# A two-layer streaming encoder: the high parts of the prompt's queries and of the differential attention's keys and values cast by POOL in place of ACT

## The chip, the core and the metric

One Trainium2 chip, of which the kernel uses one core. A core has TensorE (PE in the profile; PEld is its loading of weights), VectorE (DVE), ScalarE (ACT), GpSimd (POOL) and a queue that issues transfers (SP). Each engine takes its own instructions in order. The metric is the device time of one execution in microseconds (us); smaller is better.

## What is computed

The reference runs two layers over 1024 prompt tokens and over 8 x 16 new tokens ("decode" below) with caches. Layer A has differential attention of 4 heads, with two score maps each, and cross-attention to 256 memory tokens; layer B has sliding-window attention with sinks and the same cross-attention. Every branch is gated, the branches go through one output projection, and a layer norm follows.

```
def diff_attend(q, k, v, mask, lam):
    s = jnp.einsum('bqhcd,bkhcd->bhcqk', q, k).astype(jnp.float32) * (DA_QK ** -0.5)
    ...
    p = jax.nn.softmax(s, axis=-1)
    a = p[:, :, 0] - lam * p[:, :, 1]
    return jnp.einsum('bhqk,bkhd->bqhd', a.astype(v.dtype), v)
```

Everything is float32, and the product must be about as precise. The kernel makes such a product from operands of a shorter type (`F32R`): an operand x is written as a high part, x cast to that type, and a low part, x minus the high part, and a product is the sum of two or three products of parts.

## The kernel before

Each operand is split by `split(hi, lo, src, eh, el)`: one engine casts `src` to `hi` (`eh`: "act" or DVE), another subtracts `hi` from `src` into `lo` (`el`: "dve" or "pool"). Weights and caches come from memory raw (`wraw`, `draw`), are cast by ACT and subtracted by DVE (`wh`/`wl`, `dkh`/`dkl`). What POOL subtracts is, above all:

- `load_q` and `mem_prompt`: the queries of one unit, loaded into `ldq` (128 x 256) and split into `qh` and `ql`; 96 such splits in a run.
- `build_head`: keys and values of a head of layer A, loaded into one of two `ldk` buffers (128 x 256). `stack_k` casts all 128 rows of a key tile into `kh` and overwrites the lower 64 rows with the low part; the values are split into the two halves of a `vh` tile.
- `layer_b_build`: the keys of layer B, also by `stack_k`, in four pieces of 64 x 512 out of two `P0` buffers; its values are split by ACT and POOL.

A unit of attention (`diff_prompt`, `mem_prompt`, `swa_prompt`) is a generator: it loads its queries, then makes scores (`sc`), exponentials (`P`, ACT), transposes (`tp`), splits those (`ah`, `al`) and multiplies by the values. `pipe` runs some 4 to 7 units in turn. Between their steps `dose` and `steps` emit background work, the projections (`pj`, three matmuls for each of 8 pieces of the contraction), and a second stream computes the decode attention (`dc`, `do`), whose queries are laid out by POOL's copies into `qc` and `qbd`.

This emission is not the final order. Class `Order` takes all instructions with their dependences, gives each a cost by a formula, and plans each engine's order with a list scheduler in four passes; `keep` fixes the best order found, engine by engine. The formula knows POOL's copies, its subtracts and that some instructions of DVE and POOL hold one another. An instruction that moves to another engine therefore changes the planned order on all of them, SP's transfers included.

Line numbers of the profile are those of the kernel before: L110 is the cast on ACT in `split`, L113 the subtract, L525 and L526 the two of `stack_k`, L184 the matmuls of the projections, L126 those of `mm`, L130 the transposes, L454 and L461 the loads of keys and values, L396 the loads of queries.

Of the kernel before, what the change touches and what calls it, by code (L numbers as in the profile page):

```python
# [64 lines left out]
class Kernel:  # L65
# [41 lines left out]
    def split(self, hi, lo, src, eh="act", el="dve"):  # L107
        nc = self.nc
        if eh == "act":
            nc.scalar.copy(hi, src)  # L110
        else:
            nc.vector.tensor_copy(hi, src)
        (nc.vector if el == "dve" else nc.gpsimd).tensor_tensor(lo, src, hi, op=ALU.subtract)  # L113
# [276 lines left out]
    def load_q(self, l, pair, t):  # L390

        self.need((("q", l), t // 3))
        x = self.t2([128, 256], "ldq").rearrange("p (a b) -> p a b", b=128)
        src = self.q[l][pair * 128:(pair + 1) * 128, t * 128:(t + 1) * 128].rearrange("(c d) t -> d c t", d=64)
        for i in range(2):
            self.nc.sync.dma_start(x[64 * i:64 * i + 64], src)  # L396
        qh, ql = self.q_tiles()
        self.split(qh, ql, x, "act", "pool")
        return [(qh[:, c], ql[:, c]) for c in range(2)]

    def load_q8(self, l, j):
# [120 lines left out]
        return [self.t2([128, 2, 128], x, F32R, bufs=2) for x in ("qh", "ql")]  # L522

    def stack_k(self, dst, x):
        self.nc.scalar.copy(dst, x)  # L525
        self.nc.gpsimd.tensor_tensor(dst[64:128], x[64:128], dst[64:128], op=ALU.subtract)  # L526


# [281 lines left out]
    def build_head(self, i):  # L810

        Kh, V = [None, None], [None, None]
        p, h = i // 2, i % 2

        def fill():
            hc = slice(h * 128, (h + 1) * 128)
            for half in (1, 0):
                if i:
                    yield from self.since(8 * i - (7 if half else 4))
                Kh[half] = self.kv_tile("kh", [128, 2, 512])  # L820
                V[half] = self.kv_tile("vh", [128, 4, 2, 128])
                for j in (0, 2):
                    t = 4 * half + j
                    self.need((("kvA", p), t + 1))
                    for c in range(2):
                        rows = slice(h * 128 + c * 64, h * 128 + c * 64 + 64)
                        x = self.load_k(("kvA", p), rows, slice(t * 128, t * 128 + 256), self.t2([128, 256], "ldk"))
                        self.stack_k(Kh[half][:, c, j * 128:j * 128 + 256], x)
                        if c:
                            yield  # L830
                    x = self.load_v(("kvA", p), t, 2, hc, self.t2([128, 256], "ldk"))
                    vt = V[half][:, j:j + 2]
                    self.split(vt[:, :, 0, :], vt[:, :, 1, :], x, "act", "pool")
                    yield

        return Kh, V, self.side(fill())
# [70 lines left out]
    def mem_prompt(self, l, h, pr, built):  # L907

        nc = self.nc
        self.phase(("m", l))  # L910
        mk, mv, build = built
        tok = slice(pr * 256, (pr + 1) * 256)
        self.need((f"mq{l}", h))
        x = self.reload_T((f"mq{l}", h), "ldq", tok)[:, 0, :]
        qh, ql = self.q_tiles()
        self.split(qh, ql, x.rearrange("p (a b) -> p a b", b=128), "act", "pool")
        yield
        while not mk:
            build.advance(1)
        sc = self.ps("sc")  # L920
        for i in range(2):
            self.mm3(sc[:, i * 256:(i + 1) * 256], qh[:, i, :], ql[:, i, :], mk[0][:, h, :], mk[1][:, h, :])
        self.dose()
        nmx = self.t2([128, 4], "nmx4", bufs=2)[:, 0:2]
        nc.vector.tensor_reduce(nmx, sc[:, 0:512].rearrange("p (a b) -> p a b", b=256), axis=AX.X, op=ALU.max, negate=True)
        P = self.t2([128, 1024], "P0")
        s = self.t2([128, 4], "s4", bufs=2)[:, 0:2]
        for i in range(2):
            nc.scalar.activation(P[:, i * 256:(i + 1) * 256], sc[:, i * 256:(i + 1) * 256], AF.Exp, bias=nmx[:, i:i + 1], accum_out=s[:, i:i + 1])
        r = self.t2([128, 4], "r4", bufs=2)[:, 0:2]  # L930
        nc.vector.reciprocal(r, s)
        for i in range(2):
            nc.scalar.activation(P[:, i * 256:(i + 1) * 256], P[:, i * 256:(i + 1) * 256], AF.Copy, scale=r[:, i:i + 1])  # L933
        yield
        build.flush()
        self.need((f"mg{l}", h))
        u = self.reload_T((f"mg{l}", h), "ldu", tok)[:, 0, :]
        ah, al = self.split_T([P[:, i * 256 + kb * 128:i * 256 + (kb + 1) * 128] for kb in range(2) for i in range(2)], 0.5)
        o = self.ps("tp")[:, 0:256]
        for kb in range(2):  # L940
            vt, q2 = mv[kb][:, h], slice(2 * kb, 2 * kb + 2)
            self.mm3(o, vt[:, 0, :], vt[:, 1, :], ah[:, q2], al[:, q2], start=(kb == 0), stop=(kb == 1))
        self.dose()
        yield
        mixp = self.t2([128, 256], "mixp")
        nc.vector.tensor_tensor(mixp, o, u, op=ALU.mult)
        nc.sync.dma_start(self.mixm[l][pr][:, h, :], mixp)
# [874 lines left out]
```

## Time and profile before

| what | value |
|---|---|
| median of 3 runs (lowest to highest) | 1151.73 us (1150.84 to 1156.75) |
| profiled execution, own time | 1155.46 us |
| its span, first to last instruction | 1153.7 us |
| mean granted TensorE clock | 0.996 of full speed |
| busy: PE / DVE / ACT / POOL | 97% / 71% / 63% / 30% of the span |

The table's last line is an average over stages: setup, the first projections and the first head's keys to about 90 us, layer A with the decode attention to about 600, output projection and norm to about 735, layer B to about 1040, and the last projection. Matmuls are pipelined and their ends are modelled, so the share of PE says little about short waits. In the rows further down, "out<-in" names tiles with their numbers left out, and a time in us counts from the start of the span.

### The profile page before, as it was taken

To read this page: it belongs to the slowest core of one execution; us is meant where nothing else is said; L and a number is where in the kernel's file an instruction comes from. 1 tells how busy PE (TensorE), PEld (TensorE's weight loads), DVE (VectorE), ACT (ScalarE), POOL (GpSimd) and SP (SyncE) were. 2 spreads that over 40 slices of the span, in tenths; PEclk is the share of its full clock that TensorE was granted. 3 is DMA by queue.
4 is the path that set the end of the run, shared out by engine and by line. 5 is a ranking of instruction groups with operands and counts; after the bars stand their busy time and mean duration, and the time that the engine had idled before them with its cause. 6 is when DMAs were issued, how large, how long until landed. Compare 5 with 4: busy or idle time off the path is not lost.

```text
span 1153.7 us, 21451 instructions
## 1 busy us (share of the span) xinstructions
PE 1118.5 (97%) x6404; PEld 992.1 (86%) x6404; DVE 821.2 (71%) x2084; ACT 728.9 (63%) x1863; POOL 349.8 (30%) x570
## 2 busy tenths in 40 slices
PE   8998999999999999999999999999999999999997
PEld 5798998789888987899778889999999999997885
DVE  4326898789999999997875488142657687675376
ACT  5327587677878887887874234332767788697111
POOL 3225434335332421221121144320323232125033
PEclk9999999999999999999999999999999999999999
DMA  8865656774787657777787654554433346678643
GB/s 281 221 177 150 185 173 192 188 228 142 233 273 223 189 181 244 220 245 222 207 258 226 231 192 141 150 146 135 150 114 118 121 141 210 200 222 243 208 167 136
DMA packets 206836, 221.67 MB, mean 192 GB/s; under 512 B 47088, under 2 KB 138224, under 8 KB 206704
## 3 DMA queue, kind: packets, MB, share of 16 engines
q1 hardware_dynamic: 206720, 220.31, 62.8%
q8 instruction: 50, 0.82, 0.3%
q14 instruction: 66, 0.54, 0.2%
HBM read 162.42 MB, written 58.72 MB: 192 GB/s over the span
## 4 chain that ended last, share of the span: by engine, by line
PE 71%; DVE 9%; DMA 8%; ACT 5%; issue 4%; SPq 1%; POOL 1%; DVEq 0%; ACTq 0%; POOLq 0%
PE pj L184 50%; PE tp L126 5%; PE sc L126 4%; PE do L126 4%; PE tp L130 4%; PE dc L126 3%; DVE dkl L113 2%; DVE wl L113 1%; DMA draw<-dk 1%; ACT ob L726 1%; DMA ldk<-kT_kvA 1%; DVE m L551 1%; DMA wraw<-wO 1%; PE dc L130 1%; DVE dP L638 1%
## 5 line engine op out<-in xcount | busy, mean ns | idle before, releaser
L184 PE MATMUL pj<-wh,th 128*128 128x512 f32 (+1 forms) x648 | 233.9, 362 | 5.9 <-ACT th L110 5.4
L184 PE MATMUL pj<-wl,th 128*128 128x512 f32 (+1 forms) x648 | 233.9, 362 | 0.2 <-POOL wl L113 0.2
L184 PE MATMUL pj<-wh,tl 128*128 128x512 f32 (+1 forms) x648 | 233.1, 360 | 0.0
L184 PE MATMUL pj<-th,wh 128*128 128x384 f32 x672 | 230.4, 343 | 0.2 <-ACT ev L374 0.2
L184 PE MATMUL pj<-th,wl 128*128 128x384 f32 x672 | 229.7, 342 | 0.0
L184 PE MATMUL pj<-tl,wh 128*128 128x384 f32 x672 | 229.0, 341 | 0.0
L113 DVE TENSOR_TENSOR dkl<-draw,dkh 128x512 fp32r<-128x512 f32 (+1 forms) x197 | 136.7, 703 | 23.6 <-ACT dkh L110 21.4
L113 POOL TENSOR_TENSOR ql<-ldq,qh 128x256 fp32r<-128x256 f32 x96 | 74.2, 777 | 248.8 <-ACT qh L110 195.3
L184 PEld LDWEIGHTS pj<-wh,th 128*128 128x128 f32 x648 | 122.3, 189 | 25.3 <-ACT th L110 5.7
L184 PEld LDWEIGHTS pj<-wl,th 128*128 128x128 f32 x648 | 122.1, 188 | 20.5 <-POOL wl L113 1.4
L110 ACT CAST wh<-wraw 128x512 fp32r<-128x512 f32 x160 | 98.6, 622 | 62.7 <-PE pj L184 40.7
L184 PEld LDWEIGHTS pj<-wh,tl 128*128 128x128 f32 x648 | 122.2, 189 | 18.6 <-DVE tl L113 0.9
L110 ACT CAST dkh<-draw 128x512 fp32r<-128x512 f32 (+1 forms) x197 | 119.6, 619 | 25.8 <-PE dc L126 8.4
L113 DVE TENSOR_TENSOR wl<-wraw,wh 128x512 fp32r<-128x512 f32 x156 | 109.8, 715 | 33.3 <-ACT wh L110 33.1
L184 PEld LDWEIGHTS pj<-th,wh 128*128 128x128 f32 x672 | 126.9, 189 | 2.4 <-ACT ev L374 0.5
L184 PEld LDWEIGHTS pj<-tl,wh 128*128 128x128 f32 x672 | 126.7, 188 | 1.8
L184 PEld LDWEIGHTS pj<-th,wl 128*128 128x128 f32 x672 | 126.8, 189 | 1.2
L126 PE MATMUL sc<-kh,qh 128*128 128x256 f32 (+2 forms) x224 | 68.9, 315 | 2.6 <-ACT P L559 1.4
L130 PE MATMUL tp<-ident,P 128*128 128x128 f32 x408 | 69.1, 275 | 1.3 <-DVE s4d L995 0.4
L126 PE MATMUL sc<-kh,ql 128*128 128x256 f32 (+2 forms) x224 | 68.1, 314 | 0.0
L559 ACT ACTIVATE P<-sc,m 128x512 f32<-128x512 f32 (+3 forms) x96 | 55.4, 581 | 8.9 <-DVE m L555 4.1
L130 PEld LDWEIGHTS tp<-ident,P 128*128 128x128 f32 x408 | 49.1, 140 | 9.5 <-ACT P L933 1.4
(235 smaller groups left out, 2369.6 us busy)
## 6 DMA issues: line engine op xcount, KB each, us to landing
draw<-dk SPq DMA_DIRECT2D x64, 256.0 KB
draw<-dv SPq DMA_DIRECT2D x64, 256.0 KB
ldq<-q SPq DMA_DIRECT2D x128, 64.0 KB
wraw<-wM SPq DMA_DIRECT2D x32, 256.0 KB
wraw<-wO SPq DMA_DIRECT2D x32, 256.0 KB
draw<-cmk SPq DMA_DIRECT2D x32, 256.0 KB
draw<-cmv SPq DMA_DIRECT2D x32, 256.0 KB
wraw<-wBT SPq DMA_DIRECT2D x24, 256.0 KB
```

Of the source, the lines that this page charges most:

```text
L110: nc.scalar.copy(hi, src)
L113: (nc.vector if el == "dve" else nc.gpsimd).tensor_tensor(lo, src, hi, op=ALU.subtract)
L126: self.last = self.nc.tensor.matmul(*args, **kw).ins.name
L130: self.last = self.nc.tensor.transpose(out, in_, self.ident[:k, :k]).ins.name
L184: ins = self.nc.tensor.matmul(*args, **kw).ins
L551: nc.vector.tensor_reduce(m2[:, i:i + 1], sc[:, :kn], axis=AX.X, op=ALU.max, negate=True)
L559: nc.scalar.activation(pt[:, 512 * i:512 * i + kn], sc[:, :kn], AF.Exp, bias=nmx, accum_out=st[:, i:i + 1])
L638: self.nc.vector.tensor_tensor_reduce(out, o, x, -1.0, TOP, ALU.add, ALU.min, nm)
L726: nc.scalar.activation(y[at], x[of], AF.Copy, scale=w[of])
```

## The change

In `split` a third choice for `eh` lets POOL make the high part. Four places use it: `load_q`, the values in `build_head`, the queries in `mem_prompt`, and (written out) `stack_k`, which layer B's keys use too. The subtract was on POOL and stays there, so POOL makes the cast and then the subtract. Nothing else in the program is edited: the splits of weights, caches, probabilities, memory keys and values, and of layer B's values are as before.

```diff
@@ -108,6 +108,8 @@
         nc = self.nc
         if eh == "act":
             nc.scalar.copy(hi, src)
+        elif eh == "pool":
+            nc.gpsimd.tensor_copy(hi, src)
         else:
             nc.vector.tensor_copy(hi, src)
         (nc.vector if el == "dve" else nc.gpsimd).tensor_tensor(lo, src, hi, op=ALU.subtract)
@@ -395,7 +397,7 @@
         for i in range(2):
             self.nc.sync.dma_start(x[64 * i:64 * i + 64], src)
         qh, ql = self.q_tiles()
-        self.split(qh, ql, x, "act", "pool")
+        self.split(qh, ql, x, "pool", "pool")
         return [(qh[:, c], ql[:, c]) for c in range(2)]
 
     def load_q8(self, l, j):
@@ -522,7 +524,7 @@
         return [self.t2([128, 2, 128], x, F32R, bufs=2) for x in ("qh", "ql")]
 
     def stack_k(self, dst, x):
-        self.nc.scalar.copy(dst, x)
+        self.nc.gpsimd.tensor_copy(dst, x)
         self.nc.gpsimd.tensor_tensor(dst[64:128], x[64:128], dst[64:128], op=ALU.subtract)
 
 
@@ -830,7 +832,7 @@
                             yield
                     x = self.load_v(("kvA", p), t, 2, hc, self.t2([128, 256], "ldk"))
                     vt = V[half][:, j:j + 2]
-                    self.split(vt[:, :, 0, :], vt[:, :, 1, :], x, "act", "pool")
+                    self.split(vt[:, :, 0, :], vt[:, :, 1, :], x, "pool", "pool")
                     yield
 
         return Kh, V, self.side(fill())
@@ -913,7 +915,7 @@
         self.need((f"mq{l}", h))
         x = self.reload_T((f"mq{l}", h), "ldq", tok)[:, 0, :]
         qh, ql = self.q_tiles()
-        self.split(qh, ql, x.rearrange("p (a b) -> p a b", b=128), "act", "pool")
+        self.split(qh, ql, x.rearrange("p (a b) -> p a b", b=128), "pool", "pool")
         yield
         while not mk:
             build.advance(1)
```

The two added lines shift every later line: from L110 on, a line of before is two lines further down afterwards (the cast in `split` on POOL is L112, the subtract L115; those of `stack_k` L527 and L528). How the planner's orders differ is shown at three places. In the names a number tells tiles apart.

The first is POOL at the start of layer A, where the first head's keys (`kh_737`, out of `ldk`) are made ready, and behind them the decode queries `qc`. Before:

```order
60 L526 TENSOR_TENSOR kh_737<-ldk_739,kh_737 64x256
61 L526 TENSOR_TENSOR kh_737<-ldk_744,kh_737 64x256
62 L677 COPY qc_154_898<-qT_150_888 64x2x32 x2
63 L677 COPY qc_155_899<-qT_151_889 64x2x32 x2
64 L676 COPY qbd_902<-qT_150_888 64x2x2x16 x2
65 L676 COPY qbd_902<-qT_151_889 64x2x2x16 x2
66 L113 TENSOR_TENSOR ql_885<-ldq_881,qh_884 128x256
```

With the change:

```order
66 L527 CAST kh_737<-ldk_739 128x256
67 L528 TENSOR_TENSOR kh_737<-ldk_739,kh_737 64x256
68 L527 CAST kh_737<-ldk_744 128x256
69 L528 TENSOR_TENSOR kh_737<-ldk_744,kh_737 64x256
70 L679 COPY qc_154_898<-qT_150_888 64x2x32 x2
71 L679 COPY qc_155_899<-qT_151_889 64x2x32 x2
72 L678 COPY qbd_902<-qT_150_888 64x2x2x16 x2
73 L678 COPY qbd_902<-qT_151_889 64x2x2x16 x2
74 L112 CAST qh_884<-ldq_881 128x256
75 L112 CAST vh_738<-ldk_749 128x2x128
76 L115 TENSOR_TENSOR ql_885<-ldq_881,qh_884 128x256
```

Each subtract has its cast in front of it, in pairs, and the copies into `qc` still come behind the same two subtracts; the query's subtract `ql_885` has a value's cast ahead of it as well.

The second is TensorE at the same time: `dc_914` are the matmuls that read `qc`, and `pj` are projections of 384 columns. Before:

```order
375 L184 MATMUL pj_1124<-th_117,wl_642 128x384
376 L126 MATMUL dc_914<-qT_150_888,qc_154_898 128x64
377 L126 MATMUL dc_914<-qT_151_889,qc_154_898 128x64
378 L184 MATMUL pj_1124<-th_117,wh_641 128x384
379 L184 MATMUL pj_1124<-tl_118,wh_641 128x384
380 L184 MATMUL pj_1124<-th_117,wl_642 128x384
381 L184 MATMUL pj_1124<-th_117,wh_641 128x384
382 L184 MATMUL pj_1124<-tl_118,wh_641 128x384
383 L184 MATMUL pj_1124<-th_117,wl_642 128x384
384 L184 MATMUL pj_1124<-th_117,wh_641 128x384
385 L126 MATMUL dc_914<-qT_150_888,qc_155_899 128x64
```

With the change, from the same row on:

```order
375 L186 MATMUL pj_1124<-th_117,wl_642 128x384
376 L186 MATMUL pj_1124<-th_117,wh_641 128x384
377 L186 MATMUL pj_1124<-tl_118,wh_641 128x384
378 L186 MATMUL pj_1124<-th_117,wl_642 128x384
379 L186 MATMUL pj_1124<-th_117,wh_641 128x384
380 L186 MATMUL pj_1124<-tl_118,wh_641 128x384
381 L186 MATMUL pj_1124<-th_117,wl_642 128x384
382 L186 MATMUL pj_1124<-th_117,wh_641 128x384
383 L186 MATMUL pj_1124<-tl_118,wh_641 128x384
384 L128 MATMUL dc_914<-qT_150_888,qc_154_898 128x64
385 L128 MATMUL dc_914<-qT_151_889,qc_154_898 128x64
```

The matmuls that read `qc_154` stand 8 projection matmuls further back.

The third is ACT in layer A, at about 305 us of the profiled execution: `ah_4276` is the high part of a transposed tile that TensorE multiplies next, `P_1051` exponentials of the next map. Before:

```order
408 L615 ACTIVATE tp_4024,ss_4252<-tp_4024 128x128
409 L110 CAST ah_4276<-tp_4271 128x512
410 L110 CAST vh_3768<-ldk_3779 128x2x128
411 L110 CAST vh_3768<-ldk_3992 128x2x128
412 L110 CAST wh_4375<-wraw_4377 128x512
413 L110 CAST wh_4408<-wraw_4410 128x512
414 L110 CAST wh_4414<-wraw_4416 128x512
415 L110 CAST qh_4648<-ldq_4645 128x256
416 L559 ACTIVATE P_1051_4510,s_1052_4511<-sc_4505,m_1049_4504 128x256
```

With the change:

```order
359 L589 ACTIVATE mixp_4249<-tp_4024,r_905_4021 128x128
360 L561 ACTIVATE P_984_4311,s_985_4312<-sc_4306,m_982_4305 128x384
361 L110 CAST ah_4276<-tp_4271 128x512
362 L561 ACTIVATE P_1051_4510,s_1052_4511<-sc_4505,m_1049_4504 128x256
363 L708 COPY xs_4146<-dc_4328 64x512
364 L617 ACTIVATE tp_4024,ss_4252<-tp_4024 128x128
```

The two value casts and the query cast are gone from ACT, three weight casts have moved elsewhere, and the exponential of `P_1051` follows `ah_4276` at once.

## Rows read from the trace of the kernel before

**Rows 1.** The page's busy time of each engine, share of the span, instructions.

```profile
PE 1118.5 (97%) x6404; PEld 992.1 (86%) x6404; DVE 821.2 (71%) x2084; ACT 728.9 (63%) x1863; POOL 349.8 (30%) x570
```

**Rows 2.** Per stretch: length, busy PE PEld DVE ACT POOL, clock, DMA share, GB/s.

```profile
100.00:600.00 500.00, 484.86 (x2830) 424.01 (x2828) 447.02 (x1239) 398.26 (x1021) 155.55 (x259) 1.00 0.70 211
...
280.00:480.00 200.00, 192.92 (x1073) 166.68 (x1072) 191.09 (x575) 170.43 (x441) 60.09 (x87) 0.99 0.70 218
...
760.00:1040.00 280.00, 278.04 (x1781) 266.65 (x1779) 180.06 (x496) 198.36 (x565) 69.39 (x132) 1.00 0.51 156
```

**Rows 3.** Waits of TensorE's weight loads, 100 to 600 us: sum, times, longest.

```profile
PEld tp L126 <- ACT ah L110: 5.9, 11, 1.5
...
PEld sc L126 <- ACT P L559: 3.3, 6, 1.6
...
PEld tp L126 <- ACT ah L606: 2.1, 3, 1.4
...
PEld dc L126 <- ACT dkh L110: 2.1, 5, 1.0
...
PEld dc L130 <- DVE dP L727: 4.2, 4, 2.2
...
PEld tp L126 <- DVE al L113: 3.4, 8, 0.7
```

**Rows 4.** ACT's instructions by shape: count, busy us, mean ns, idle before.

```profile
L110 ACT CAST qh<-ldq 128x256 fp32r<-128x256 f32 x96 | 38.5, 407 | 22.5 <-PE sc L126 9.1 <-DMA ldq<-q 7.4 <-issue 4.6
...
L525 ACT CAST kh<-ldk 128x256 fp32r<-128x256 f32 x32 | 12.5, 406 | 9.8 <-DMA ldk<-kT_kvA 9.8
...
L110 ACT CAST vh<-ldk 128x256 fp32r<-128x256 f32 x16 | 6.4, 406 | 3.8 <-DMA ldk<-v_kvA 3.8
```

**Rows 5.** 100 to 600 us: qh (PE, PEld, ACT, POOL), ldk (ACT, POOL).

```profile
100.00:600.00 500.00, 44.02 (x150) 27.06 (x150) 17.83 (x44) 35.90 (x44) 1.00 0.70 211
...
100.00:600.00 500.00, 14.23 (x37) 31.06 (x37) 1.00 0.70 211
```

**Rows 6.** POOL's copies and DVE's subtracts: min/median/max ns; then DVE's by shape.

```profile
L677 POOL CAST qc<-qT x32: 229/234/1272, 90.9 to 409.4; 64x64 fp32r<-64x64 f32 x32
...
L731 POOL COPY Pn<-Pn x8: 196/270/715, 127.5 to 518.0; 128x16 f32<-128x16 f32 x8
...
L113 DVE TENSOR_TENSOR dkl<-draw,dkh x197: 443/684/1550, 18.1 to 1047.9; 128x512 fp32r<-128x512 f32 x194, 128x432 fp32r<-128x432 f32 x2, 128x288 fp32r<-128x288 f32 x1
...
L113 DVE TENSOR_TENSOR dkl<-draw,dkh 128x512 fp32r<-128x512 f32 x194 | 134.3, 701 | 23.5 <-ACT dkh L110 21.4 <-DMA ldu<-pre_mg_T 0.5 <-DMA om<-ob 0.3
...
L113 DVE TENSOR_TENSOR wl<-wraw,wh 128x512 fp32r<-128x512 f32 x156 | 109.8, 715 | 33.3 <-ACT wh L110 33.1
```

**Rows 7.** Start of layer A: chain, POOL's and TensorE's timeline, busy time behind it.

```profile
86.39 2.29 DMA ldk<-kT_kvA
...
89.24 1.59 POOL L526 TENSOR_TENSOR kh<-ldk,kh 64x256 fp32r<-64x256 f32 x2 [3.63 <-ACT kh L525]
...
90.89 1.07 POOL L677 CAST qc<-qT 64x64 fp32r<-64x64 f32 x4
...
91.45 0.41 PE L126 MATMUL dc<-qT,qc 128*128 128x64 f32 x2 [2.81 <-POOL qc L677]
...
92.70:96.00 3.30, 3.30 (x11) 2.75 (x9) 0.89 (x4) 1.94 (x5) 3.10 (x6) 0.50 0.30 80
```

**Rows 8.** Start of layer B: chain, TensorE's timeline, POOL's key subtracts.

```profile
750.34 0.96 POOL kh L526
...
751.30 4.82 DMA P<-ropeT
...
770.76 32.30 PE pj L184 x186
...
768.22 0.30 PE L126 MATMUL sc<-kh,qh 128*128 128x128 f32 x1 [1.05 <-ACT qh L110]
...
L526 POOL TENSOR_TENSOR kh<-P,kh x4: 1289/1294/1470, 747.8 to 751.6; 64x512 fp32r<-64x512 f32 x4
```

## The prediction

> **What bounds the kernel now.** I read the page's busy shares first, then the table by stage, then the waits of TensorE, and last the chain at the two places where a stage begins. TensorE is busy 97% of the span [rows 1], but its ends are modelled, so the share hides short waits. By stage [rows 2] the picture splits. From 760 to 1040 us (layer B) TensorE is busy 278.04 of 280 us: what other engines do there can hardly move the end. From 100 to 600 us (layer A with the decode work woven in) it is busy 484.86 of 500, and two other engines are close behind: DVE 447.02 and ACT 398.26, against POOL's 155.55. Between 280 and 480 us DVE is at 191.09 of 200 us, so DVE is as full as TensorE there, and ACT is at 170.43. The waits of TensorE's weight loads in 100 to 600 us [rows 3] say who comes last: the four longest that ACT ends sum to 5.9 + 3.3 + 2.1 + 2.1 = 13.4 us, the two longest of DVE to 4.2 + 3.4 = 7.6 us. So ACT is the engine most often late, DVE the one with least room. The change takes from ACT and gives to POOL; the question is whether POOL's new work costs DVE.
>
> **What moves, and its price.** ACT loses 96 casts of the prompt's queries (38.5 us), 32 of the keys (12.5) and 16 of the values (6.4) [rows 4], 57.4 us, and four wider key casts in layer B besides. POOL gets all of them. No row shows POOL casting 256 columns from 32 bits. Below, it can't be cheaper than POOL's cast of 64 columns, 229 ns at its shortest; above, it has one input where POOL's subtract of as many columns has two, and two of those take 1.59 us [rows 7], 0.80 each. The line through POOL's copy of 16 columns (196 ns) and its cast of 64 (229 ns) [rows 6] climbs 33 ns over 48 columns, 0.69 ns each, and gives 229 + 192 x 0.69 = 361 ns. I take 0.36 us: 144 x 0.36 = 52 us, and about 0.54 us for each of the four wide ones, 54 us in all, so POOL goes from 350 to some 404 us. A high part is thus made about as fast as on ACT (406 ns a cast), only on another engine.
>
> **Term 1: ACT's relief, -2.7 us.** In 100 to 600 us, 44 query casts (17.83 us) and 37 key and value casts (14.23) leave ACT [rows 5], 32.1 of its 398.26. Its load falls from 0.80 to 0.73. If the 13.4 us of waits [rows 3] fall with the load, by 8%, that is 1.1 us; if they fall like busy over idle time (0.80/0.20 = 3.9 to 0.73/0.27 = 2.7, by 31%) it is 4.2 us. I take 2.7, between them; the ends are 0 (DVE is late just behind ACT, as it can be between 280 and 480 us) and 4.2. The piece of ACT's order shown under the change is how this comes about: behind `ah_4276`, whose kind TensorE waits for most, ACT had two value casts, three weight casts and a query cast before its next exponential; now that exponential is next.
>
> **Term 2: the start of layer A, -1.4 us.** At 88.6 us TensorE runs into `dc_914` and waits 2.81 us for the `qc` copies on POOL, which stand behind two key subtracts [rows 7]; after it the granted clock is 0.50 for 3.3 us, the lower of the two levels (1.2 GHz). On POOL before: the keys' load ends at 86.39 + 2.29 = 88.68, ACT casts, the two subtracts run from 89.24 to 90.83, the copies follow. With the change, from about 88.8: two casts and two subtracts in a row, 2 x 0.36 + 1.59 = 2.31, to 91.1, so `qc` is ready some 0.3 us later. But TensorE's new order puts 8 more projection matmuls ahead of `dc_914`; at 32.30 / 186 = 0.174 us each [rows 8] they fill 1.4 us of the hole. The work moved ahead is taken from later, so it is a gain only as long as later has no hole for it, and the weave has such work throughout. Ends: -3.1, if the slower clock goes too (half of 3.3 us), and +1.0, if the loads of keys and values slip: they have two buffers, SP's next load waits for the subtract that frees one, and a pair of casts now stands on POOL in front of it (0.7 us a pair, where ACT made one while POOL subtracted).
>
> **Term 3: DVE held by POOL, +1.3 us.** DVE's subtract `dkl` takes 684 ns in the median and 1550 at most [rows 6]; POOL's 64-column cast 234 and 1272: each is now and then held by the other. The price over the whole run: 194 `dkl` with a mean of 701 lose 17 ns each, 3.3 us; 156 `wl` of the same shape with a mean of 715 lose 31 each, 4.8 us. So 8.1 us of DVE's time for 350 us of POOL's, 2.3%; 54 us more cost 1.3 us, and as DVE has no room between 280 and 480 us I count all of it. Ends: 0, and what the first rival says.
>
> By the Trainium skill (SBUF — State Buffer, section Who interferes with whom) a DVE instruction with two SBUF inputs and a GpSimd instruction that reads SBUF share a read interface, and whichever comes second is fully blocked until the other ends. The two maxima agree with it. Taken as the price, it would cost a meeting the rest of a cast, and the sum would then be the first rival's and not this one's; the measured mean is far below.
>
> **Term 4: the start of layer B, +0.4 us.** There POOL's four 512-column key subtracts (1.29 us each) are on the chain, and with them the release of the buffers that the rotary tables are loaded into (4.82 us), at whose end TensorE waits 1.05 us for a query's cast [rows 8]. Two casts of 0.54 stand in front of the first pair, where one ACT cast (two of the 406 ns ones at most, as it has twice the columns) stood ahead of it: the first buffer comes free 0.3 to 0.5 us later, and the second, behind four casts, 1.4. I take 0.4; ends 0 (the load of the tables may stand behind another transfer in SP's order) and 1.4.
>
> **At nothing:** the change issues no DMA itself. The query casts in layer B (TensorE full there; without that cover they would gain a little of ACT's time), and the wait of POOL's queue on loads: a cast that waits for its load now holds POOL's queue, where before the subtract behind it held it just as long, waiting for ACT.
>
> **Sum:** -2.7 - 1.4 + 1.3 + 0.4 = -2.4 us. The profiled execution took 1155.46 us, 3.7 above the median of the three runs; it would go to 1153.1, and a median of 1151.73 to 1149.3.
>
> **The rivals.** A difference under about 0.5% (5.8 us) can't be told from none, so the forecast is "no change": chance 0.42.
> *Slower: POOL's casts block DVE.* Place: 100 to 600 us, above all 280 to 480, where a DVE delay goes straight into TensorE's waits. If each of the 81 casts there holds a subtract for half its length, 0.18 us, DVE loses 14.6 us; with terms 1, 2 and 4 the sum is -2.7 - 1.4 + 0.4 + 14.6 = +10.9, 1162.6. It decides from a mean hold of (5.8 + 3.7) / 81 = 0.12 us. For it: the maxima of [rows 6]. Against it: POOL works already 155.55 of these 500 us, and a `dkl` loses 17 ns in the mean. Chance 0.22.
> *Faster: ACT's lateness was the cause of more.* If half of the 13.4 us go, and the start of layer A gains its 3.1, then -6.7 - 3.1 + 1.3 + 0.4 = -8.1, 1143.6. It decides from 4.4 us of those waits gone, a third. For it: ACT ends more of TensorE's waits than DVE does, and DVE's own waits on ACT shrink too; ACT no longer waits at the head of its queue for keys that are being loaded. Against it: DVE's 191.09 of 200. Chance 0.36.
>
> All engines' orders are remade by the planner, which adds a few us to either side. The likeliest time is 1149.3. The range for 8 in 10 goes from 1137 to 1161, across both rivals' times but for the slow one's last; the forecast's own is 1146 to 1157.5. The chances of faster, the same and slower are those of the three cases: 0.36, 0.42, 0.22.
>
> **What would show it.** ACT busy near 669 and POOL near 404 us; 144 casts of 256 columns on POOL near 0.36 us; `dkl` with a mean under 0.71; the wait ahead of `dc` near 91 us about 1.4 us long; the waits on `ah` and `P` in 100 to 600 us shorter by a fifth. A `dkl` mean above 0.75, or TensorE waiting for POOL's `qh`, `ql` or `kh` for some us, would prove me wrong on the slow side; waits on `ah` halved, on the fast side.

## The result: slower by 0.9%, outside the range

| kernel | median | lowest to highest | runs |
|---|---|---|---|
| before, beside it | 1153.12 us | 1150.84 to 1156.75 | 4 |
| with the change | 1164.99 us | 1162.48 to 1166.38 | 4 |

The ratio is 1.0089 with a 95% interval of 1.0067 to 1.0111, some 10 us (the two medians stand 11.9 us apart, which lies within it). The profiled execution took 1165.36 us. Below are the lines of its profile that answer to the rows of before. First the page's busy times [rows 1]:

```profile
PE 1120.1 (96%) x6404; PEld 991.9 (85%) x6404; DVE 833.9 (72%) x2084; ACT 683.6 (59%) x1715; POOL 423.8 (36%) x718
```

The instructions moved as the change says: 148 from ACT to POOL. ACT lost 45.3 us of busy time; the rows that left it sum to some 60, but ACT's instructions overlap a little in the records, and busy time counts such stretches once. POOL gained 74.0. DVE has the same 2084 instructions and is busy 12.7 us longer: they got slower.

The windows of [rows 2], and below them 300 to 400 us, of after; columns as there:

```profile
100.00:600.00 500.00, 478.46 (x2791) 418.97 (x2790) 447.83 (x1226) 368.63 (x927) 197.46 (x340) 1.00 0.70 208
280.00:480.00 200.00, 189.06 (x1051) 160.38 (x1051) 192.23 (x569) 154.37 (x395) 77.09 (x126) 1.00 0.69 210
760.00:1040.00 280.00, 276.79 (x1762) 265.62 (x1761) 183.26 (x486) 179.96 (x506) 95.24 (x182) 1.00 0.51 154
...
300.00:400.00 100.00, 92.85 (x497) 77.42 (x497) 94.43 (x276) 73.47 (x187) 41.95 (x68) 1.00 0.74 226
```

The same 100 us of before:

```profile
300.00:400.00 100.00, 97.86 (x546) 87.30 (x546) 95.47 (x288) 85.34 (x222) 33.56 (x45) 0.98 0.75 232
```

TensorE is busy 6.4 us less in layer A's 500 us, and 5.0 of these are lost between 300 and 400, where DVE was full before the change and still is. TensorE runs 497 matmuls there instead of 546, and DVE 276 instructions in 94.4 us instead of 288 in 95.5; as the order was remade, they aren't the same ones. ACT has 26 us of room there now and nothing comes of it. Layer B's 280 us lose another 1.3. The granted clock is 1.00 in all four rows of the changed kernel (the full level, 2.4 GHz).

The waits of TensorE's weight loads from 100 to 600 us, as in [rows 3] (ACT's cast in `split` keeps its line number, L110; `ah` of L606 is now L608):

```profile
PEld tp L128 <- DVE al L115: 6.3, 12, 2.0
PEld tp L128 <- ACT ah L110: 4.1, 6, 1.7
PEld tp L132 <- ACT tp L617: 3.7, 3, 2.1
PEld tp L128 <- ACT ah L608: 3.1, 3, 1.8
PEld do L128 <- DVE dP L115: 2.7, 4, 1.0
PEld tp L132 <- DVE P L574: 2.6, 3, 1.5
...
PEld sc L128 <- ACT P L561: 2.0, 6, 0.7
```

The four longest that ACT ends sum to 12.9 us against 13.4, the two longest of DVE to 9.0 against 7.6. Some of ACT's waits shrank (`ah` of L110 5.9 to 4.1, `P` 3.3 to 2.0) and others of ACT came in their place (`ah` of L608 2.1 to 3.1, `tp` 1.3 to 3.7).

The casts on POOL and DVE's two large subtracts by shape [rows 4, 6], busy us and mean ns behind the bar:

```profile
L112 POOL CAST qh<-ldq 128x256 fp32r<-128x256 f32 x96 | 43.2, 451 | 206.3 <-PE sc L128 181.0 <-issue 10.1 <-DMA ldq<-q 9.1
L527 POOL CAST kh<-ldk 128x256 fp32r<-128x256 f32 x32 | 16.5, 518 | 24.5 <-DMA ldk<-kT_kvA 24.4
L112 POOL CAST vh<-ldk 128x256 fp32r<-128x256 f32 x16 | 9.6, 602 | 13.7 <-DMA ldk<-v_kvA 10.2 <-PE tp L128 3.4
L115 DVE TENSOR_TENSOR dkl<-draw,dkh 128x512 fp32r<-128x512 f32 x194 | 137.6, 718 | 24.0 <-ACT dkh L110 17.6 <-PE dc L128 3.1 <-DMA mixm<-mixp 1.0
L115 DVE TENSOR_TENSOR wl<-wraw,wh 128x512 fp32r<-128x512 f32 x156 | 110.6, 719 | 37.0 <-ACT wh L110 35.1 <-DMA ldu<-pre_gs_T 1.4
```

The same casts as one tile's instructions (shortest, median, longest ns):

```profile
L112 POOL CAST qh<-ldq x96: 387/397/901, 91.3 to 1044.3; 128x256 fp32r<-128x256 f32 x96
...
L527 POOL CAST kh<-ldk x32: 390/398/1832, 67.5 to 410.0; 128x256 fp32r<-128x256 f32 x32
...
L527 POOL CAST kh<-P x4: 611/616/959, 755.2 to 760.1; 128x512 fp32r<-128x512 f32 x4
```

A cast of a query takes 0.397 us in the median (0.36 was predicted); means of 0.451 to 0.602 and a longest one of 1.832 say that some of POOL's casts are held, too. With the four wide ones they come to 72 us, not 54.

The start of layer A in the timeline (start, us; in brackets the wait ahead and what ended it), with the window behind it, as in [rows 7]:

```profile
88.93 1.18 POOL L679 CAST qc<-qT 64x64 fp32r<-64x64 f32 x4
...
89.79 0.30 PE L128 MATMUL dc<-qT,qc 128*128 128x64 f32 x2
...
95.52 0.67 PE L128 MATMUL sc<-kh,qh 128*128 128x512 f32 x1 [1.82 <-POOL kh L528]
...
92.70:96.00 3.30, 1.48 (x8) 1.07 (x7) 1.99 (x4) 0.84 (x2) 3.15 (x6) 0.95 0.16 52
```

The wait of 2.81 us ahead of `dc` is gone, and the stretch of half clock behind it too (0.95 in the same window, against 0.50). A wait of 1.82 us for a key on POOL has come 4 us later.

The start of layer B, POOL's key splits, as in [rows 8]:

```profile
755.17 1.17 POOL L527 CAST kh<-P 128x512 fp32r<-128x512 f32 x2 [2.51 <-DMA P<-kT_kvB]
756.42 2.73 POOL L528 TENSOR_TENSOR kh<-P,kh 64x512 fp32r<-64x512 f32 x2
...
759.21 1.52 POOL L527 CAST kh<-P 128x512 fp32r<-128x512 f32 x2
760.81 3.01 POOL L528 TENSOR_TENSOR kh<-P,kh 64x512 fp32r<-64x512 f32 x2
```

TensorE runs through projections there, and no wait for these keys shows.

### The profile page after: what moved, and what is told of

The parts are those of the page before. It is cut to its first block, busy times and chain, and to the rows that moved or that the text cites. A ratio compares the mean times of both kernels' runs of the same rounds, so it can differ in the third digit from the quotient of the medians.

```text
span 1163.6 us, 21390 instructions
## 1 busy us (share of the span) xinstructions
PE 1120.1 (96%) x6404; PEld 991.9 (85%) x6404; DVE 833.9 (72%) x2084; ACT 683.6 (59%) x1715; POOL 423.8 (36%) x718
## 4 chain that ended last, share of the span: by engine, by line
PE 56%; DVE 16%; DMA 5%; ACT 4%; issue 3%; SPq 1%; POOL 0%; DVEq 0%; ACTq 0%; POOLq 0%
PE pj L186 41%; PE tp L128 4%; PE tp L132 3%; PE do L128 3%; PE sc L128 3%; DVE wl L115 2%; DVE dkl L115 2%; PE dc L128 2%; DVE m L553 2%; DVE al L115 1%; DVE dP L729 1%; ACT dkh L110 1%; DMA wraw<-wAT 1%; DMA draw<-dv 1%; DVE P L574 1%
## 5 line engine op out<-in xcount | busy, mean ns | idle before, releaser
L115 DVE TENSOR_TENSOR dkl<-draw,dkh 128x512 fp32r<-128x512 f32 (+1 forms) x197 | 140.3, 721 | 26.3 <-ACT dkh L110 20.0
L110 ACT CAST dkh<-draw 128x512 fp32r<-128x512 f32 (+1 forms) x197 | 119.0, 618 | 42.8 <-PE dc L128 19.7
L115 DVE TENSOR_TENSOR wl<-wraw,wh 128x512 fp32r<-128x512 f32 x156 | 110.6, 719 | 37.0 <-ACT wh L110 35.1
L110 ACT CAST wh<-wraw 128x512 fp32r<-128x512 f32 x160 | 97.9, 621 | 66.2 <-PE pj L186 42.2
L112 POOL CAST qh<-ldq 128x256 fp32r<-128x256 f32 x96 | 43.2, 451 | 206.3 <-PE sc L128 181.0
L115 POOL TENSOR_TENSOR ql<-ldq,qh 128x256 fp32r<-128x256 f32 x96 | 75.5, 787 | 7.0 <-PE sc L128 1.0
```

Of the source, the lines that this page charges most:

```text
L112: nc.gpsimd.tensor_copy(hi, src)
```

## The experiments

Three explanations stood against each other. **Hold:** POOL's casts read the state buffer (SBUF, the memory on the chip that all tiles but TensorE's accumulators lie in) while DVE's subtracts do, and stop them, so DVE, full from 300 to 400 us, falls behind. **Lateness:** the casts stand in front of POOL's own subtracts and make POOL late, whatever they read. **Draw:** moved instructions make the planner plan all engines' orders anew; orders differ in quality by chance, and the new one happens to be worse than the one of before. Hold and lateness together are the casts' own price.

**The engine and the order, one without the other.** In the first kernel the planner is told that the casts are on ACT; TensorE, DVE, SP and the rest of ACT then keep the order of before row for row, and each cast goes to POOL right in front of its subtract. In the second the planner is told POOL, and the casts run on ACT: all other work stands in the changed order.

```diff
+        self.engine = [2 if i.name in moved else e for i, e in zip(self.ins, self.engine)]
...
+        seqs[2] = [i for i in seqs[2] if self.ins[i].name not in self.moved]
+        for i in cast:
+            lo = next(j for j in self.succ[i] if self.engine[j] == 3)
+            seqs[3].insert(seqs[3].index(lo), i)
```

(2 is ACT, 3 POOL. The second kernel has the two numbers exchanged, `nc.scalar.copy` for the cast, and puts it into ACT's order by its planned start.)

> The 148 casts run on POOL, each right in front of its subtract, but the planner is told that they are on ACT, so that PE, DVE, SP and the rest of ACT keep the order of before, row for row. If the casts themselves cost the time (POOL holding DVE's subtracts, or a longer way to each low part), this takes about as much as the changed kernel: 8 to 12 us over before, ratio 1.007 to 1.010. If the remade order costs it, this is as fast as before or a little faster: -3 to +2 us, 0.997 to 1.002. If both, about half: 1.004 to 1.005.

> The casts run on ACT, at the place of their planned start, and the planner is told that they are on POOL, so that PE, DVE, SP and the rest of POOL have the order of the changed kernel, row for row. If the casts on POOL cost the time, this is near before, 0.998 to 1.003. If the remade order costs it, it stays 8 to 12 us over before, 1.007 to 1.010; if both, 1.004 to 1.006.

Measured: 1.0122 (1.0105 to 1.0139) for the casts on POOL in the old order, 1.0117 (1.0099 to 1.0136) for the casts on ACT in the new one. The pages, first to second:

```profile
PE 1122.2 (96%) x6404; PEld 995.0 (85%) x6404; DVE 833.5 (71%) x2084; ACT 684.9 (59%) x1715; POOL 432.0 (37%) x718
```

```profile
PE 1123.4 (96%) x6404; PEld 991.4 (85%) x6404; DVE 828.6 (71%) x2084; ACT 730.3 (63%) x1863; POOL 348.9 (30%) x570
```

Both lie above every case that was named for them, and each alone costs at least as much as both together: 14.1 and 13.5 us against 10.3 (the intervals overlap).

The first shows that the casts have a price when nothing else moves: DVE is busy 12.3 us longer. As its order is that of before, each matmul can be set beside itself in the two traces (my reading of the starts): it is 3.9 us later than in before at 100 us, 2.8 at 300, 7.3 at 400, 7.7 at 750, 10.5 at 800 and 12.7 at the end. Most of the time goes where DVE is full, from 300 to 400 us, and at the start of either layer, where TensorE waits for POOL itself:

```profile
PE sc L128 <- POOL kh L528: 3.6, 1, 3.6
PE sc L128 <- POOL qh L112: 2.3, 1, 2.3
```

The second shows that an order planned for casts on POOL is bad for casts on ACT. It also shows that much of what was seen in the changed kernel needs no cast on POOL. DVE is busy 7.4 us longer than in before, so of the 12.7 us of the changed kernel only 5.3 come in between the two kernels of the new order. And from 300 to 400 us TensorE runs 496 matmuls, as few as the 497 of the changed kernel, and DVE the same 276 instructions:

```profile
300.00:400.00 100.00, 94.34 (x496) 79.35 (x496) 92.36 (x276) 82.17 (x212) 29.47 (x47) 0.98 0.74 228
```

The two prices don't add, so an order and the engine it was planned for belong together, and this pair leaves open how good either order is.

**The planner's draw.** `WAKE` is a cost of the planner's formula, 45 ns. Set to 46 it describes the same kernel about as well, and the orders come out different in many places.

```diff
-    LANDING, RATE, ISSUE, WAKE = 2200.0, 17.0, 460.0, 45.0
+    LANDING, RATE, ISSUE, WAKE = 2200.0, 17.0, 460.0, 46.0
```

The same line was set to 42, 43, 44, 47, 48 and 49 in both kernels, before and changed.

> The kernel before with one number of the planner nudged (the wake-up of an engine 46 ns for 45), which remakes the orders without moving any work. If the remade order alone can cost what the change cost, this scatters by several us (0.994 to 1.010); if orders from this planner are about equally good, it stays within 3 us of before (0.997 to 1.003).

> The changed kernel with the same nudge. If the casts on POOL cost the time whatever the order, ratio 1.006 to 1.012 again; if the changed kernel only drew a bad order, it may come out anywhere from 0.996 to 1.010.

> The kernel before with the planner's wake-up number at 44 ns for 45: another draw of an order for unmoved work. If the order of before is a lucky draw and the change only lost it, this is 3 to 8 us over before (1.003 to 1.007), like the draw at 46. If the draw at 46 was the exception, it is within 3 us (0.997 to 1.003).

> The changed kernel at 44 ns. If the casts on POOL cost nothing of their own, draws of the changed kernel and of the kernel before spread over the same range, 1.003 to 1.009 here. If the casts cost 4 us or more of their own, it lies above the draw of before at 44 by that: 1.007 to 1.012.

> The kernel before at 47 ns, as at 44: 1.003 to 1.007 if the order of before was a lucky draw, 0.997 to 1.003 if not.

> The changed kernel at 47 ns, as at 44: 1.003 to 1.007 if the casts cost nothing of their own, 1.007 to 1.012 if they cost 4 us or more.

> A fifth draw of an order for the kernel before (48 ns). The four so far lie at 1.006, 1.000, 1.005 and 0.999; if that is scatter of the planner, this lies in 0.998 to 1.008.

> A fifth draw for the changed kernel. The four so far lie at 1.008, 1.009, 1.007 and 1.000, and above their partners by 2, 10, 2 and 1 us. If the casts have a price of their own of some 2 us, this is 0 to 5 us above the draw of before at 48; if their price is that of the measured change, 8 to 12 us above it.

> The kernel before with the planner's waking cost at 43 ns instead of 45. Earlier draws of before (44, 46, 47, 48 ns) stood at 1.0060, 1.0053, 0.9991, 1.0019. Both theories: 0.999 to 1.007.

> The changed kernel at 43 ns. Own price of the casts: 3 to 8 us above its partner (ratio of the pair 1.003 to 1.007). The draw alone: as often below its partner as above, within 6 us; DVE's busy time as the partner's. Own price by the hold: DVE's busy time 2 us or more above the partner's.

> The kernel before at 49 ns: 0.999 to 1.007 by both theories.

> The changed kernel at 49 ns: as at 43 ns, 3 to 8 us above its partner by the own price, either side of it by the draw alone.

> The kernel before at 42 ns: 0.999 to 1.007 by both theories.

> The changed kernel at 42 ns: 3 to 8 us above its partner by the casts' own price, either side of it by the draw alone; by the hold DVE is busy for 2 us or more longer than in its partner.

All ratios are to the kernel before at 45, on the same chip; the half width of their intervals is 0.0013 to 0.003. The difference is that of the two ratios times 1154 us.

| WAKE | before | changed | difference, us | DVE busy, before | DVE busy, changed |
|---|---|---|---|---|---|
| 42 | 1.0045 | 1.0087 | +4.8 | 827.1 | 831.1 |
| 43 | 1.0047 | 1.0032 | -1.7 | 820.4 | 832.1 |
| 44 | 1.0060 | 1.0079 | +2.2 | 826.0 | 830.6 |
| 45 | 1 | 1.0089 | +10.3 | 821.2 | 833.9 |
| 46 | 1.0053 | 1.0074 | +2.4 | 824.0 | 828.3 |
| 47 | 0.9991 | 0.9997 | +0.7 | 821.9 | 823.5 |
| 48 | 1.0019 | 1.0043 | +2.8 | 818.8 | 830.4 |
| 49 | 1.0027 | 1.0011 | -1.8 | 818.6 | 828.5 |
| mean | 1.0030 | 1.0052 | +2.5 | 822.3 | 829.8 |

The kernel before, unchanged but for that constant, spreads from 0.9991 to 1.0060; the changed one from 0.9997 to 1.0089. The eight differences have a mean of +2.5 us with a 95% interval of -0.8 to +5.7 (standard deviation 3.9, 8 pairs); the seven without the pair at 45 have +1.3 (-0.9 to +3.6). The measured +10.3 is the largest of them: the order of before at 45 lies 3.5 us under the mean of its eight, that of the changed kernel 4.3 above the mean of its own. 3.5 + 4.3 + 2.5 = 10.3, so by this reckoning three quarters of the loss is the draw. The three must add up, and each of the two means is uncertain by 1 to 1.5 us (standard error), so the shares are rough. Whether 45 was once chosen because its order ran well isn't on record; if so, before is a selected draw, and any new order would have lost that much.

Against what was expected, before scattered at 44 and 46, ran as at 45 at 47, and lay in the range given at the other four. A price of 3 us or more over the partner came out at 42 alone; 44, 46, 47 and 48 show 0.7 to 2.8, and 43 and 49 lie below their partners. DVE, however, is busy longer with the change in all eight pairs, by 1.6 to 12.7 us, 7.5 in the mean. How much longer says little of the time: over the eight pairs the two differences have a correlation of 0.14.

The page and the window from 280 to 480 us of the changed kernel at 47:

```profile
PE 1119.6 (97%) x6404; PEld 995.7 (86%) x6404; DVE 823.5 (71%) x2084; ACT 684.7 (59%) x1715; POOL 427.1 (37%) x718
...
280.00:480.00 200.00, 193.15 (x1069) 166.07 (x1068) 193.56 (x581) 162.08 (x408) 78.00 (x125) 0.99 0.71 217
```

The 144 casts of 256 columns take as long on POOL (69.5 us in all, 69.3 at 45), DVE is busy 1.6 us longer than in its partner, and TensorE does its 193 us of work in this stretch, as in [rows 2]. So there is an order in which the casts cost next to nothing; that they meet fewer of DVE's instructions in it is likely, and not shown.

**Reading or not.** To price the casts without any new order, the kernel before got 148 idle instructions on POOL, one in front of each of the subtracts in question, with all planned orders as they were. In one kernel they are copies of 256 columns from a constant tile into a spare one, in the other fills of the same spare tile, which read nothing. Nobody uses the result.

```diff
+        self.added.append(nc.gpsimd.tensor_copy(y, self.ident.unsqueeze(1).broadcast_to([128, n // 128, 128])).ins.name)
```

```diff
+        self.added.append(nc.gpsimd.memset(y, 1.0).ins.name)
```

> The kernel before, casts on ACT and all orders as before, with 148 idle copies on POOL added, 256 columns from a constant tile to a spare tile that nobody reads, one in front of each of the subtracts. It adds POOL's time and its holding of DVE, and takes nothing from ACT. If POOL's copies hold DVE where it is full, as the rival of the prediction has it, 6 to 11 us over before (1.005 to 1.010). If they cost what the means of before say, 1 to 3 us (1.000 to 1.003).

> The same with fills (memset, which read nothing) in the place of the copies. If it is the reading that holds DVE, this is 1 to 3 us over before at most (0.998 to 1.003) while the copies cost more; if it is POOL's time in front of each subtract, it costs nearly what the copies cost.

Measured: copies 1.0084 (1.0069 to 1.0100), +9.7 us; fills 1.0032 (1.0017 to 1.0047), +3.7 us. The page of the copies and the idle instruction itself:

```profile
PE 1121.4 (96%) x6404; PEld 993.5 (85%) x6404; DVE 831.5 (72%) x2084; ACT 730.1 (63%) x1863; POOL 419.8 (36%) x718
...
L112 POOL COPY idle<-ident x148: 388/399/1145, 63.4 to 1045.0; 128x256 f32<-128x256 f32 x148
```

The page of the fills and theirs:

```profile
PE 1117.5 (97%) x6404; PEld 993.0 (86%) x6404; DVE 822.7 (71%) x2084; ACT 729.9 (63%) x1863; POOL 392.7 (34%) x718
...
L112 POOL MEMSET idle<- x148: 302/312/472, 62.1 to 1037.3; 128x256 f32 x148
```

The copies cost DVE 10.3 us, and one of them takes 1.145 us; the fills cost DVE 1.5, and none takes over 0.472. Hold and lateness are both real: the copies cost 6.0 us more than the fills, and the fills' own price is clear of noise, with DVE only 1.5 us longer. Where it arises isn't seen; in the one profiled execution TensorE with the fills is never over 1.7 us behind before. Against what was expected, the copies came out as the rival *Slower* had it, and the fills just above the case of reading (0.998 to 1.003). A fill is shorter than a copy (0.312 against 0.399 us in the median); if lateness goes with POOL's time, the copies' share of it is 3.7 x 0.399 / 0.312 = 4.7 us, and 5.0 of the 9.7 are left for the hold.

The planner doesn't know of this hold. In `schedule` some instructions of DVE keep all of POOL's from starting, and a subtract of POOL keeps those of DVE from starting; a copy or a cast of POOL keeps back nothing of DVE's (`held`). So no order here was planned around it. A formula that knows it, and the change planned by that, was not run.

Which of DVE's instructions pay is seen in two that write `mixp` and in `al`. Of before (shortest, median, longest ns):

```profile
L588 DVE SCALAR_TENSOR_TENSOR mixp<-tp,r,mixp x32: 262/342/352, 132.2 to 508.1; 128x128 f32<-128x128 f32 x32
...
L622 DVE SCALAR_TENSOR_TENSOR mixp<-mixp,rr,ldu x32: 310/344/776, 138.9 to 518.7; 128x128 f32<-128x128 f32 x32
...
L607 DVE SCALAR_TENSOR_TENSOR al<-tp,ah x62: 667/691/693, 507.4 to 1057.9; 128x512 fp32r<-128x512 f32 x62
```

Of the changed kernel:

```profile
L590 DVE SCALAR_TENSOR_TENSOR mixp<-tp,r,mixp x32: 264/337/352, 129.8 to 516.6; 128x128 f32<-128x128 f32 x32
...
L624 DVE SCALAR_TENSOR_TENSOR mixp<-mixp,rr,ldu x32: 304/348/1265, 142.4 to 526.8; 128x128 f32<-128x128 f32 x32
...
L609 DVE SCALAR_TENSOR_TENSOR al<-tp,ah x62: 666/684/693, 513.9 to 1067.6; 128x512 fp32r<-128x512 f32 x62
```

Operation and shape of the two `mixp` are the same. The one with `tp`, TensorE's accumulator, among its inputs never exceeds 0.352 us, nor does `al`, which reads `tp` too, go above 0.693; the one with both inputs in the state buffer goes to 1.265. By the Trainium skill (SBUF — State Buffer, section Who interferes with whom) a DVE instruction with two SBUF inputs contends with a GpSimd instruction that reads SBUF, not with one that only writes it. These rows and the two idle kernels agree with that. That no other instruction of DVE is held is not what the traces show: its cast `vn`, with one input, in the state buffer, goes far beyond its median too, in before and beside the idle copies:

```profile
L112 DVE CAST vn<-draw x10: 404/416/862, 101.7 to 887.6; 16x512 fp32r<-16x512 f32 x10
...
L121 DVE CAST vn<-draw x10: 405/415/1558, 104.4 to 896.1; 16x512 fp32r<-16x512 f32 x10
```

## Why the prediction was wrong

**The step that failed** is the sentence that the planner's remade orders add "a few us to either side". It stood at the end, outside the sum, and moved neither the chances nor the forecast. The table gives its size: a kernel's draws have a standard deviation of 2.9 us (before) and 4.1 us (changed), and the one order that everything was compared with was a good draw, 3.5 us under its mean. The prediction took that order's time for the time of "the kernel before". With the changed kernel's bad draw, 4.3 above its mean, that makes 7.8 of the 10.3 us by the reckoning above. The new order with the casts back on ACT, 13.5 us over before, says too that an order by itself can cost as much as the change did.

**Term 3, DVE held by POOL (+1.3), was mis-sized.** DVE's busy time rose by 7.5 us in the mean of eight pairs and by 12.7 in the pair that was predicted; where the order stayed, by 12.3 with the casts (old order), 5.3 (new order) and 10.3 with idle copies. What that costs at the end was measured in the old order alone, about 5 us by the estimate from copies and fills. Three things were too small in it. The casts come to 72 us, not 54. The price per POOL time was read from `dkl` and `wl` alone, 244 us of DVE's work [rows 6], while other instructions with two inputs from the state buffer pay as well. And in the changed kernel `dkl` and `wl` rose by only 3.3 + 0.8 us of the 12.7, so the tests set for it, a `dkl` mean above 0.75 or under 0.71, decided nothing: the mean went from 701 to 718. The other sign of the slow side, TensorE waiting for POOL's keys, showed once, for 1.82 us. The rival *Slower* named a mechanism that is there, with 0.18 us a cast and 81 casts in layer A; measured is 0.051 us for each of 148 in the mean of the pairs (7.5 / 148) and 0.086 here. That its 1162.6 us came near the measured 1164.99 is in good part luck, as most of the difference is the draw.

**Term 1, ACT's relief (-2.7), is not seen.** ACT's busy time fell by 45 us, to 683.6 and not 669, and its four longest waits went from 13.4 to 12.9. The waits on `P` and on `ah` of L110 did fall by more than the fifth that was named, but those on `ah` of L608 rose (both `ah` together 8.0 to 7.2), and TensorE waited more for DVE (`al` 3.4 to 6.3), which the prediction had as this term's lower end, 0.

**Term 2, the start of layer A (-1.4), came true in its sign, in part by a mechanism that it had wrong:** the 2.81 us wait and the half clock are gone. The 8 projection matmuls stand ahead of `dc` as it said. But the copies into `qc` started 2 us earlier (88.93 against 90.89), where they were to be 0.3 later, since the last keys ahead of them came sooner: their cast starts at 87.65 us, right behind their load, which in before ended at 88.68. SP issues these loads from 83.28 us on and not from 84.60, in its own remade order; that was luck for this term. TensorE's work is some 1 to 3 us ahead of before from 100 to 175 us (my reading of the time at which equal work is done in both traces), and level again by some 200 us.

**Term 4, the start of layer B (+0.4),** shows no cost in the changed kernel. In the old order there is one, of another kind: TensorE waits 2.3 us for a query's cast on POOL where it waited 1.05 for ACT's.

**The sum without the draw** was -2.4 us; the pairs say +2.5 (-0.8 to +5.7). The forecast of -2.4 lies outside that interval too, but "no change within 0.5%" is what the edit itself does over many orders, as far as these runs can tell. The measured kernel is slower, and the forecast was of that kernel.

What stays open is the sign of the edit's own price: the interval of eight pairs holds zero. Also open is why draws at 43 and 49 lose 10 to 12 us of DVE's busy time and no time at all, while the one at 45 loses both. None of the nineteen other kernels clearly beats the one before; the nearest, 0.9991 and 0.9997, can't be told from it.

## What to carry to other kernels

Where a planner or a scheduler orders the work, a change's effect is the difference of two draws: nudge a constant that should not matter, on both sides, before any step of the difference is explained. Work moved to POOL can be paid for on DVE where DVE subtracts or combines two tiles from the state buffer, so count all such instructions and look at their longest durations, not at the mean of one kind; and fix the order to price it. Taking work from the engine that TensorE most often waited for gained nothing here, where the next engine was already full.

## What the hardware showed beyond that

A POOL copy of 256 columns of 32 bits takes 0.399 us in the median, a cast of as many to the shorter type 0.397, a fill 0.312. 148 such copies in front of POOL's subtracts made DVE's unchanged instructions 10.3 us longer, 148 fills 1.5 us. Held instructions reach far beyond their median on both sides: a cast of 0.398 us took 1.832, a DVE instruction of 0.348 took 1.265.
